# Returned splits tied behind weight casts, one quarter transposed on TensorE, later loads of x and norm rows in a hybrid GLA/Hyena block

## The chip, the core and the metric

The kernel runs on one core of a Trainium2 chip. The metric is the device time of one execution in microseconds (us). Engines are named as in the profile: PE (TensorE), DVE (VectorE), ACT (ScalarE), POOL (GpSimd) and SP (SyncE). Each works through its own instructions in the order in which the program holds them. SP, ACT and POOL also issue DMA transfers.

## The reference

One encoder layer on 256 tokens of width 2048, all in float32. Cut to what matters:

```python
proj = h @ w_in                                  # 2048 -> q, k, v, r, gates, Hyena input, merge gates
y_gla = gla_branch(q, k, v, r, ...)              # gated linear attention in both directions, 4 heads
y_hy = hyena_branch(hy_u, ...)                   # short convolution, then two gated FFT convolutions
g = sigmoid(gate_logits).reshape(B, L, 2, D)
merged = g[:, :, 0] * (y_gla @ w_gla_o) + g[:, :, 1] * (y_hy @ w_hy_o)
h = layernorm(ALPHA * h + merged @ w_out, ln1_g, ln1_b)
ff = square(relu(h @ w_ff1)) @ w_ff2             # 2048 -> 8192 -> 2048
out = layernorm(ALPHA * h + ff, ln2_g, ln2_b)
```

## The kernel before

**Weights.** All weights stream from DRAM in blocks of 128x2048 floats (1 MB). `fetch` (L115) asks for a block on SP's queue (`raw`, three buffers) and splits each of its two halves into a high part (`whi`, a cast on ACT, L108) and a low part (`wlo`, a subtraction on DVE, L109). `whi` and `wlo` have three half-block buffers each, so a cast can run at most one and a half blocks ahead of PE. Activations are split in the same way, and each product is made of three: high x high, high x low, low x high. One block is 24 matmuls of 128x512 for both halves of the tokens. Four blocks are a group (`token_group`, L215) of 512 output columns. Where the result is to lie with channels on the partitions, two blocks make a `channel_pair` (L175).

**Side work.** `later(d, fn)` (L135) notes that `fn` is to be written out `d` blocks from now. `pump` (L139), which comes after each block, writes out what is due, and `drain` (L147) all that is left. So the lines of Hyena, GLA and of the returned data stand between those of the weight blocks. The framework's scheduler then orders each engine's instructions by a plan of its own, unless a dependency fixes it.

**Returns from DRAM.** A matmul's output has tokens on the partitions; the next one needs channels there. `turn_blocks` (L202) transposes 32x32 squares on DVE, `bounce_out` (L205) writes the tile to DRAM and `bounce_in` (L210) reads it back in four DMAs so that the squares land in place; both are on POOL's queue. Then the returned tile is split by a cast on ACT and a subtraction on DVE, `split_hi_lo` (L107). This is done in GLA (`gla_back`, L612), in Hyena (`turned`, L681, with `hy_v`, `hy_out`), for the merged tensor (L826 to L838, `back_split` L821) and for the MLP's hidden tensor f (`ff1`, L1020).

**Stages in order.** Opening and the Hyena filters (`filt_time`, `filt_freq`, beside the products of q, k and r); GLA (beside v and the first merge gate, g1); Hyena in eight channel groups, each with three channel pairs uv, ux and uz, and the output products of GLA, go, in between; the second merge gate, g2; the return of Hyena's result (L815) and its output product ho, which merges into m; the transposed m, mT, times w_out: the groups wo0 to wo3, of which the last runs in an order written out by hand together with the first norm (L961 to L1010); then the MLP, ff1 in four quarters f0 to f3 and ff2, w2, one quarter behind; the second norm and the store.

In Hyena, `hy_fwd` and `hy_mul` make a group's spectrum, multiply it by the filter T, read from DRAM, and split the product into Yh and Yl; `hy_inv` multiplies these with the inverse transform (yp).

**The seam between ho and wo.** `zr` holds x for the residual (z1) and two norm rows. It takes the memory of `yh`, ho's operand, so it is loaded after ho: x in one DMA (L846), two rows of the norm, each spread over all partitions (L851), all on ACT's queue. Each of ho's four groups is multiplied by the gate and added (L832, L833), turned and sent through DRAM. wo0 needs all four quarters, the last one in its fourth block.

Of the kernel before, what the change touches and what calls it, by code (L numbers as in the profile page):

```python
# [10 lines left out]
F32 = mybir.dt.float32  # L11
# [6 lines left out]
P = 128  # L18
# [41 lines left out]
def block_kernel(  # L60
# [45 lines left out]

    def split_hi_lo(hi, lo, src):  # L107
        nc.scalar.copy(hi, src)  # L108
        nc.vector.tensor_tensor(lo, src, hi.bitcast(F32), op=ALU.subtract)  # L109

    nblk = wblk.shape[0]
# [294 lines left out]
    def filt_freq(c, o):  # L406
        def run():
            hh, hl = fst.pop(("h", c, o))

            def transform(r):  # L410
                pt = psum_side(f"F{r}{c}{o}").rearrange("p (a b) -> p a b", a=2)
                for i in range(2):
                    mm3(pt[:, i], dfth[:, 2 * r + i], dftl[:, 2 * r + i], hh[:, r, i], hl[:, r, i], True, True)
                return pt

            t = fp.tile([P, 2, 2, CW], F32, tag="T", name=f"T{c}{o}")
            odd = fp.tile([P, 2, CW], F32, tag="odd", name=f"odd{c}{o}")
            even = transform(0)
            nc.scalar.copy(odd, transform(1))
            nc.vector.tensor_tensor(t[:, 0], even, odd, op=ALU.add)  # L420
# [191 lines left out]
    def gla_back(h, ib):  # L612
# [3 lines left out]
        def run():  # L616
            src = sg.rearrange("p a (k j) -> p k a j", k=4)
            dst = [yT[:, 4 * h:4 * h + 4, i, ib * P:(ib + 1) * P].rearrange("p k (a j) -> p k a j", a=4)
                   for i in range(2)]
            split_hi_lo(dst[0], dst[1], src)  # L620
        return run
# [23 lines left out]
    for g in range(4):  # L645
        pss = token_group(xT, f"g1_{g}")
        for tb in range(NT):
            sig = nc.scalar.activation(m_part(g, tb), pss[tb], AF.Sigmoid)
            dep = mybir.DependencyInfo(mybir.DependencyClass.NoSync, mybir.DependencyReason.DATA)
            tc.add_manual_dep(sig.ins, last_norm[0].ins.name, dep, reason="one table change")  # L650
        for h, ib in ((g, 0), (g, 1)):
# [46 lines left out]
    def hy_v(c):  # L698
        def run():
            zh, zl = z_tiles(f"{c}0")  # L700
            sg = cst.pop(("v", c))
            for tb in range(NT):
                hi, lo = (t[:, tb].rearrange("p (c a j) -> p c a j", c=2, a=4) for t in (zh, zl))
                split_hi_lo(hi, lo, sg[:, tb::2])
            cst[("z", c, 0)] = (zh, zl)
# [39 lines left out]
    def hy_inv(c, o):  # L745
        def run():
# [15 lines left out]
            else:  # L762
                cst[("y", c)] = turned([py.rearrange("p (k b i) -> p b k i", k=4, b=4)], f"y{c}", "sg")
        return run
# [24 lines left out]
    for c in range(NCH):  # L789
        ps = channel_pair(xT, f"uv{c}")  # L790
        cst[("v", c)] = turned(by_parity(short_conv(ps, 2 * c, f"cv{c}", "cv", 2)), f"v{c}", "sg")
        later(3, hy_v(c))
        later(4, hy_fwd(c, 0))
        later(4, hy_mul(c, 0))
        ps = channel_pair(xT, f"ux{c}")
        cst[("x1", c)] = turned(by_parity(short_conv(ps, 16 + 2 * c, f"cx{c}", "cv", 2)), f"x{c}", "x1")
        later(5, hy_inv(c, 0))
        later(6, hy_fwd(c, 1))
        later(6, hy_mul(c, 1))
        ps = channel_pair(xT, f"uz{c}")  # L800
        cst[("x2", c)] = short_conv(ps, 32 + 2 * c, f"cz{c}", "cz", 2)
        later(7, hy_inv(c, 1))
        later(9, hy_out(c))
        for _ in range(go_after[c]):
            gla_o_group()


    g2_sb = qp.tile([P, NT, D], F32, tag="G", name="g2_sb")
# [5 lines left out]
    yhT = act_tile(base, "yT", "yh")  # L814
    for c in range(NCH):  # L815
        yr = hp.tile([P, 2, L], F32, tag="cv", bufs=2, name=f"yr{c}")
        nc.gpsimd.dma_start(yr, yh_dram[c])
        split_hi_lo(yhT[:, 2 * c:2 * c + 2, 0], yhT[:, 2 * c:2 * c + 2, 1], yr)
    mT = act_tile(base, "xT", "mT")

    def back_split(dst, sg):  # L821
        src = sg.rearrange("p a (k j) -> p k a j", k=4)
        hi, lo = (dst[:, :, i].rearrange("p k (a j) -> p k a j", a=8) for i in range(2))
        split_hi_lo(hi, lo, src)

    for g in range(4):  # L826
        pss = token_group(yhT, f"ho{g}")
# [17 lines left out]
    z1 = zr[:, 0:2]  # L845
    nc.scalar.dma_start(z1, x.rearrange("(a p) d -> p a d", p=P))  # L846

    def load_rows(i0):
        rows = zr[:, 2:4]
        for i in range(2):  # L850
            nc.scalar.dma_start(rows[:, i, :], ln_rows[i0 + i:i0 + i + 1, :].broadcast_to([P, D]))  # L851
        return rows
# [43 lines left out]
    st1 = ep.tile([P, NT, 8, 6], F32, tag="bst", bufs=2, name="bst1")  # L896
    rows1 = load_rows(0)

# [121 lines left out]
    def ff1(qi):  # L1020
# [12 lines left out]
        for g in range(1 if qi == 0 else 0, 4):  # L1033
# [200 lines left out]
```

## Time and profile before

| | |
|---|---|
| median of three runs | 1846.69 us (1844.93 to 1849.45) |
| profiled execution: time, span | 1849.45 us, 1847.4 us |
| PE, DVE, ACT, POOL busy | 1822.5, 1285.9, 896.4, 178.4 us |
| mean granted TensorE clock | 0.995 |
| DMA moved | 403.27 MB, 218 GB/s over the span |

A row of a timeline gives start, time, engine, line, operation and tiles; a bracket holds the engine's idle time before it and what ended that. In a table of stretches each engine has its busy time and, behind it, its count of instructions. Matmuls overlap in the pipeline, so the mean time of one in the profile is longer than the distance between two.

### The profile page before, as it was taken

What the parts mean: (1) busy time and instruction counts of PE and PEld (TensorE: products, weight loads), DVE (VectorE), ACT (ScalarE), POOL (GpSimd) and SP (SyncE); (2) the same over time, 40 slices, a digit from 0 to 9 for tenths busy, and PEclk for the clock granted to TensorE, in tenths of its full rate; (3) what the DMA queues carried; (4) which work ended last, traced back from release to release, by engine and by line L of the source; (5) the groups of instructions that cost most, each with busy time, mean ns of one, the idle gap of its engine ahead of it and who ended that gap; (6) DMA issues with size and microseconds to landing.
All of it is one profiled execution on the core that took longest, in us unless ns stands there. A gap on an engine that the chain in (4) does not pass through costs nothing.

```text
span 1847.4 us, 23213 instructions
## 1 busy us (share of the span) xinstructions
PE 1822.5 (99%) x8924; PEld 1529.2 (83%) x8924; DVE 1285.9 (70%) x1659; ACT 896.4 (49%) x1120; POOL 178.4 (10%) x317
## 2 busy tenths in 40 slices
PE   9999999999999999999999899999999999999998
PEld 7888888888888888888888688888888878888887
DVE  6889878965898988988456566566555555565567
ACT  5556567654554555455444444444434443444332
POOL 1000000120121211211001000011100100010000
PEclk9999999999999999999999999999999999999999
DMA  8677654575666666657557763677756765666553
GB/s 293 219 252 272 242 199 151 191 242 187 226 224 220 231 225 214 236 214 251 206 210 239 279 235 127 206 247 236 242 186 209 241 211 184 225 230 225 184 198 119
DMA packets 73631, 403.27 MB, mean 218 GB/s; under 512 B 10928, under 2 KB 13776, under 8 KB 34096
## 3 DMA queue, kind: packets, MB, share of 16 engines
q1 hardware_dynamic: 47376, 324.03, 49.6%
q0 software_dynamic: 19376, 58.62, 10.3%
q10 hardware_dynamic: 6768, 19.14, 3.0%
q8 instruction: 70, 1.15, 0.2%
q14 instruction: 41, 0.34, 0.1%
HBM read 370.82 MB, written 30.93 MB: 217 GB/s over the span
## 4 chain that ended last, share of the span: by engine, by line
PE 78%; DMA 3%; DVE 3%; issue 3%; ACT 1%; POOL 1%; DVEq 0%; ACTq 0%; POOLq 0%
PE w L93 18%; PE f L93 17%; PE g L93 9%; PE ux L93 5%; PE uz L93 5%; PE uv L93 5%; PE go L93 5%; PE v L93 4%; PE wo L93 3%; PE r L93 1%; DMA back<-tr_f 1%; DMA tr_m<-mt 1%; PE Zp L93 1%; PE yp L93 1%; PE ho L93 1%
## 5 line engine op out<-in xcount | busy, mean ns | idle before, releaser
L109 DVE TENSOR_TENSOR wlo<-raw,whi 128x1024 fp32r<-128x1024 f32 (+2 forms) x603 | 725.9, 1208 | 432.1 <-ACT whi L108 425.1
L108 ACT CAST whi<-raw 128x1024 fp32r<-128x1024 f32 (+2 forms) x603 | 627.1, 1042 | 709.6 <-PE w L93 184.0
L93 PE MATMUL w<-whi,f 128*128 128x512 f32 x960 | 296.6, 389 | 1.4 <-ACT whi L108 1.3
L93 PE MATMUL f<-whi,hT 128*128 128x512 f32 x960 | 296.1, 389 | 0.0
L93 PEld LDWEIGHTS w<-whi,f 128*128 128x128 f32 x960 | 180.1, 188 | 39.5 <-ACT whi L108 2.2
L93 PEld LDWEIGHTS f<-whi,hT 128*128 128x128 f32 x960 | 180.2, 188 | 37.4
L93 PE MATMUL w<-wlo,f 128*128 128x512 f32 x480 | 187.0, 389 | 1.4 <-DVE wlo L109 1.4
L93 PE MATMUL f<-wlo,hT 128*128 128x512 f32 x480 | 186.9, 389 | 0.1
L93 PE MATMUL g<-whi,xT 128*128 128x512 f32 x512 | 158.7, 390 | 0.0
L93 PEld LDWEIGHTS g<-whi,xT 128*128 128x128 f32 x512 | 96.1, 188 | 19.8
L93 PEld LDWEIGHTS w<-wlo,f 128*128 128x128 f32 x480 | 90.1, 188 | 20.9 <-DVE wlo L109 2.3
L93 PEld LDWEIGHTS f<-wlo,hT 128*128 128x128 f32 x480 | 90.1, 188 | 19.1 <-DVE wlo L109 0.5
L93 PE MATMUL g<-wlo,xT 128*128 128x512 f32 x256 | 99.7, 390 | 0.0
L93 PE MATMUL r<-whi,xT 128*128 128x512 f32 x256 | 81.4, 391 | 0.0
L93 PE MATMUL v<-whi,xT 128*128 128x512 f32 x256 | 80.1, 391 | 0.0
L93 PE MATMUL go<-whi,yg 128*128 128x512 f32 x256 | 80.1, 390 | 0.0
L93 PE MATMUL ho<-whi,yh 128*128 128x512 f32 x256 | 79.0, 389 | 0.0
L93 PE MATMUL wo<-whi,mT 128*128 128x512 f32 x208 | 66.9, 401 | 7.5 <-ACT whi L108 3.9
L93 PE MATMUL ux<-xT,whi 128*128 128x512 f32 x256 | 65.3, 393 | 0.0
L93 PE MATMUL uz<-xT,whi 128*128 128x512 f32 x256 | 64.8, 392 | 0.0
L93 PE MATMUL uv<-xT,whi 128*128 128x512 f32 x256 | 64.0, 392 | 0.0
L207 POOL DMA_DIRECT2D tr_f<-work x15 | 10.9, 725 | 529.2 <-DVE work L203 529.2
(321 smaller groups left out, 2835.3 us busy)
## 6 DMA issues: line engine op xcount, KB each, us to landing
raw<-wblk SPq DMA_DIRECT2D x302, 1024.0 KB, 4.9
w<-w4s ACTq DMA_DIRECT2D x16, 512.0 KB, 3.5
Td<-T POOLq DMA_DIRECT2D x16, 512.0 KB, 3.9
Tl<-Td POOLq DMA_DIRECT2D x16, 512.0 KB, 4.3
tr_f<-work POOLq DMA_DIRECT2D x15, 512.0 KB, 3.8
back<-tr_f POOLq DMA_DIRECT2D x60, 128.0 KB, 3.7
zr<-ln_rows ACTq DMA_DIRECT2D x4, 1024.0 KB, 13.2
raw<-wblk SPq DMA_DIRECT2D x11, 256.0 KB, 7.4
```

The source lines that it names most:

```text
L93: return eng.tensor.matmul(*args, **kw)
L108: nc.scalar.copy(hi, src)
L109: nc.vector.tensor_tensor(lo, src, hi.bitcast(F32), op=ALU.subtract)
L207: nc.gpsimd.dma_start(td.rearrange("t p x -> p t x"), st)
```

## The change

1. `split_hi_lo` takes `held`. A held split's cast on ACT is tied behind the last weight cast that has been written out so far (`last_cast`): an order within ACT's own instructions, without a semaphore. Held are the splits of data that return from DRAM: GLA's, Hyena's v, Hyena's result, the merged tensor's and f's. The last two are due after three blocks instead of two.
2. The last quarter of the merged tensor, from ho3, no longer goes through DRAM. Eight 128x128 transposes on PE put it into PSUM, and a split from there makes mT.
3. x is loaded in four column quarters, three blocks apart, and the norm rows eight blocks in, each tied behind the last weight cast.
4. Delays in Hyena: forward transforms due after 5 and 7 blocks (4 and 6 before), the output after 11 (9 before); `cz` has three buffers, the returned y its own (`sgy`), the filter tile T two. Hyena's result is read back during g2, not after it.

```diff
+    def behind(ins, other):
+        if other is not None:
+            dep = mybir.DependencyInfo(mybir.DependencyClass.NoSync, mybir.DependencyReason.DATA)
+            tc.add_manual_dep(ins.ins, other.ins.name, dep, reason="in order")
...
+    def split_hi_lo(hi, lo, src, held=False):
+        cast = nc.scalar.copy(hi, src)
+        if held:
+            behind(cast, last_cast[0])
         nc.vector.tensor_tensor(lo, src, hi.bitcast(F32), op=ALU.subtract)
+        return cast
...
-            split_hi_lo(hi, lo, raw[:, h * 1024:(h + 1) * 1024])
+            last_cast[0] = split_hi_lo(hi, lo, raw[:, h * 1024:(h + 1) * 1024])
...
-            t = fp.tile([P, 2, 2, CW], F32, tag="T", name=f"T{c}{o}")
+            t = fp.tile([P, 2, 2, CW], F32, tag="T", bufs=2, name=f"T{c}{o}")
...
-        later(4, hy_fwd(c, 0))
-        later(4, hy_mul(c, 0))
+        later(5, hy_fwd(c, 0))
+        later(5, hy_mul(c, 0))
...
-        later(6, hy_fwd(c, 1))
-        later(6, hy_mul(c, 1))
+        later(7, hy_fwd(c, 1))
+        later(7, hy_mul(c, 1))
...
-        later(9, hy_out(c))
+        later(11, hy_out(c))
...
+    def y_back(c):
+        yr = hp.tile([P, 2, L], F32, tag="cv", bufs=2, name=f"yr{c}")
+        nc.gpsimd.dma_start(yr, yh_dram[c])
+
+        def run():
+            split_hi_lo(yhT[:, 2 * c:2 * c + 2, 0], yhT[:, 2 * c:2 * c + 2, 1], yr, held=True)
+        later(2, run)
...
+    for c in range(NCH):
+        later(max(c, 2 * c - 5) + 2, lambda c=c: y_back(c))
...
-    for g in range(4):
+    for g in range(3):
         pss = token_group(yhT, f"ho{g}")
...
-        later(2, lambda g=g, sg=sg: back_split(mT[:, 4 * g:4 * g + 4], sg))
+        later(3, lambda g=g, sg=sg: back_split(mT[:, 4 * g:4 * g + 4], sg))
+    pss = token_group(yhT, "ho3")
     drain()
+    for tb in range(NT):
+        with tc.high_priority():
+            gp2 = g2_sb[:, tb, 1536:]
+            mp = m_part(3, tb)
+            nc.vector.tensor_tensor(gp2, gp2, pss[tb], op=ALU.mult)
+            nc.vector.tensor_tensor(mp, mp, gp2, op=ALU.add)
+            pt = psum_side(f"mt3{tb}")
+            for k in range(4):
+                nc.tensor.transpose(pt[:, k * P:(k + 1) * P], mp[:, k * P:(k + 1) * P], ident)
+            hi, lo = (mT[:, 12:16, i, tb * P:(tb + 1) * P] for i in range(2))
+            split_hi_lo(hi, lo, pt.rearrange("p (k x) -> p k x", k=4))
...
-    nc.scalar.dma_start(z1, x.rearrange("(a p) d -> p a d", p=P))
+
+    def load_z(g):
+        cs = slice(g * 512, (g + 1) * 512)
+        behind(nc.scalar.dma_start(z1[:, :, cs], x[:, cs].rearrange("(a p) d -> p a d", p=P)), last_cast[0])
+
+    for g in range(4):
+        later(3 * g, lambda g=g: load_z(g))
...
-    rows1 = load_rows(0)
+    rows1 = zr[:, 2:4]
+    later(8, lambda: load_rows(0))
...
-            later(2, lambda g=g, sg=sg, f=f: back_split(f[:, 4 * g:4 * g + 4], sg))
+            later(3, lambda g=g, sg=sg, f=f: back_split(f[:, 4 * g:4 * g + 4], sg))
```

The order on ACT at the seam before; `whi161` is the first block of wo0, `mg` a returned quarter of the merged tensor, `zr` x and the rows:

```order
L108 CAST mT_8868<-mg2_9322 128x4x256
L108 CAST whi161_0_9403<-raw161_9401 128x1024
L108 CAST whi161_1_9407<-raw161_9401 128x1024
L108 CAST whi162_0_9437<-raw162_9435 128x1024
L846 DMA zr_9490<-x 128x2x2048
L854 ACT_TABLE_LOAD
L851 DMA zr_9490<-ln_rows 128x2048 x2
L108 CAST whi162_1_9441<-raw162_9435 128x1024
L108 CAST whi163_0_9503<-raw163_9501 128x1024
L108 CAST whi163_1_9507<-raw163_9501 128x1024
```

The same place of the changed kernel; `mt30` and `mt31` are the two halves of the last quarter in PSUM:

```order
L115 CAST whi161_1_9405<-raw161_9399 128x1024
L115 CAST mT_8868<-mg2_9322 128x4x256
L115 CAST whi162_0_9437<-raw162_9435 128x1024
L115 CAST whi162_1_9441<-raw162_9435 128x1024
L115 CAST whi163_0_9502<-raw163_9500 128x1024
L115 CAST mT_8868<-mt30_9471 128x4x128
L115 CAST whi163_1_9506<-raw163_9500 128x1024
L877 DMA zr_9492<-x 128x2x512
L115 CAST mT_8868<-mt31_9480 128x4x128
L888 ACT_TABLE_LOAD
L115 CAST whi164_0_9537<-raw164_9535 128x1024
```

The third quarter's cast has moved behind one more weight block, the last quarter's cast is fed from PSUM, and where x and both rows stood there is one quarter of x.

On PE in the changed kernel, the transposes stand among wo0's products, after 26 of them (the two rows ahead of them are the 25th and 26th); before, wo0 has no other work in it here:

```order
L93 MATMUL wo0_0_9498<-whi162_0_9437,mT_8868 128x512
L93 MATMUL wo0_1_9499<-whi162_0_9437,mT_8868 128x512
L864 MATMUL mt30_9471<-ident_71,m1_3525 128x128 x4
L93 MATMUL wo0_0_9498<-wlo162_0_9438,mT_8868 128x512
L93 MATMUL wo0_0_9498<-whi162_0_9437,mT_8868 128x512
L93 MATMUL wo0_1_9499<-wlo162_0_9438,mT_8868 128x512
```

Ten products of wo0 lie between the four transposes of `mt30` and those of `mt31`.

In the MLP, ACT's order before, around the return of f2's first group (`f2<-back`) and the relu of its second (`work<-f21`):

```order
L108 CAST whi232_0_12244<-raw232_12242 128x1024
L108 CAST whi232_1_12248<-raw232_12242 128x1024
L108 CAST f2_12055<-back_10319 128x4x256
L108 CAST whi233_0_12280<-raw233_12278 128x1024
L108 CAST whi233_1_12284<-raw233_12278 128x1024
L1037 ACTIVATE work_10318<-f21_0_12206 128x512
```

and after:

```order
L115 CAST whi232_0_12249<-raw232_12247 128x1024
L115 CAST whi232_1_12253<-raw232_12247 128x1024
L115 CAST whi233_0_12283<-raw233_12281 128x1024
L115 CAST whi233_1_12287<-raw233_12281 128x1024
L115 CAST f2_12060<-back_10324 128x4x256
L1072 ACTIVATE work_10323<-f21_0_12211 128x512
```

The returned cast has moved behind the two casts of one more weight block and stands right ahead of the next relu.

More of the change, by code (lines that the diff above doesn't have):

```diff
@@ L619, in run @@
                    for i in range(2)]
-            split_hi_lo(dst[0], dst[1], src)
+            split_hi_lo(dst[0], dst[1], src, held=True)
         return run
@@ L648, in block_kernel @@
             sig = nc.scalar.activation(m_part(g, tb), pss[tb], AF.Sigmoid)
-            dep = mybir.DependencyInfo(mybir.DependencyClass.NoSync, mybir.DependencyReason.DATA)
-            tc.add_manual_dep(sig.ins, last_norm[0].ins.name, dep, reason="one table change")
+            behind(sig, last_norm[0])
         for h, ib in ((g, 0), (g, 1)):
@@ L703, in run @@
                 hi, lo = (t[:, tb].rearrange("p (c a j) -> p c a j", c=2, a=4) for t in (zh, zl))
-                split_hi_lo(hi, lo, sg[:, tb::2])
+                split_hi_lo(hi, lo, sg[:, tb::2], held=True)
             cst[("z", c, 0)] = (zh, zl)
@@ L762, in run @@
             else:
-                cst[("y", c)] = turned([py.rearrange("p (k b i) -> p b k i", k=4, b=4)], f"y{c}", "sg")
+                cst[("y", c)] = turned([py.rearrange("p (k b i) -> p b k i", k=4, b=4)], f"y{c}", "sgy")
         return run
@@ L813, in block_kernel @@
     drain()
[L814 to L818, printed above, removed]
     mT = act_tile(base, "xT", "mT")
@@ L823, in back_split @@
         hi, lo = (dst[:, :, i].rearrange("p k (a j) -> p k a j", a=8) for i in range(2))
-        split_hi_lo(hi, lo, src)
-    for g in range(4):
+        split_hi_lo(hi, lo, src, held=True)
+    for g in range(3):
         pss = token_group(yhT, f"ho{g}")
@@ L850, in load_rows @@
         for i in range(2):
-            nc.scalar.dma_start(rows[:, i, :], ln_rows[i0 + i:i0 + i + 1, :].broadcast_to([P, D]))
+            behind(nc.scalar.dma_start(rows[:, i, :], ln_rows[i0 + i:i0 + i + 1, :].broadcast_to([P, D])), last_cast[0])
         return rows
```

6 lines of the change are left out of this document (3 added, 3 removed).

## The prediction, made before the run

> **What bounds it.** I read the page's busy table first, then the engines' busy time by stretches of 50 us, then who waited for whom on PE, then the timelines of PE and ACT at the places where PE stood still.
>
> ```profile
> PE 1822.5 (99%) x8924; PEld 1529.2 (83%) x8924; DVE 1285.9 (70%) x1659; ACT 896.4 (49%) x1120; POOL 178.4 (10%) x317
> ```
>
> PE is busy for 99% of the span, so only three things can shorten it: fewer matmuls, PE's few stops, or a slow PE clock. The change drops no matmul. So I look for stops. In the stretches below the bracket behind PE's busy time is the count of matmuls, and PEclk is the granted clock.
>
> ```profile
> core 0: us, PE busy (x) PEld busy (x) DVE busy (x) ACT busy (x) POOL busy (x), PEclk, DMA share, GB/s
> 200.00:250.00 50.00, 48.52 (x233) 40.08 (x232) 34.51 (x39) 25.25 (x29) 2.14 (x4) 1.00 0.66 234
> 1000.00:1050.00 50.00, 43.71 (x181) 34.35 (x180) 28.34 (x30) 18.67 (x18) 6.10 (x10) 0.97 0.82 296
> 1050.00:1100.00 50.00, 48.61 (x207) 40.13 (x208) 31.38 (x35) 23.73 (x24) 0.00 (x0) 0.97 0.58 210
> 1200.00:1250.00 50.00, 50.00 (x223) 41.40 (x222) 32.40 (x33) 24.44 (x26) 6.83 (x11) 1.00 0.70 239
> 1450.00:1500.00 50.00, 49.05 (x214) 39.62 (x213) 28.23 (x28) 22.41 (x24) 7.04 (x12) 1.00 0.74 233
> 1500.00:1550.00 50.00, 48.02 (x211) 39.13 (x210) 24.88 (x23) 18.75 (x19) 0.00 (x0) 1.00 0.59 191
> ```
>
> 1200:1250 is an undisturbed stretch of 128x512 products: 223 of them. 1000:1050 gets through 42 fewer, 1050:1100 through 16 fewer, both at a clock of 0.97; 1450:1500 lacks 9 and 1500:1550 lacks 12. These products are all of one shape, so a missing count is lost time. The chain of waits gives the price of one:
>
> ```profile
> 1308.82 87.04 PE w L93 x384
> ```
>
> 87.04/384 is 0.227 us. 1000:1100 therefore loses 58 x 0.227 = 13.2 us, and 1450:1550 21 x 0.227 = 4.8 us. PE's timeline has the stops themselves:
>
> ```profile
> 1041.15 1.22 PE L93 MATMUL wo<-whi,mT 128*128 128x512 f32 x2 [2.76 <-ACT whi L108]
> 1047.10 0.73 PE L93 MATMUL wo<-whi,mT 128*128 128x512 f32 x2 [1.13 <-ACT whi L108]
> 1051.39 0.80 PE L93 MATMUL wo<-whi,mT 128*128 128x512 f32 x1 [3.56 <-ACT mT L108]
> 1507.78 0.73 PE L93 MATMUL w<-whi,f 128*128 128x512 f32 x2 [1.27 <-ACT whi L108]
> 1041.00:1046.00 5.00, 4.78 (x12) 3.07 (x12) 1.23 (x1) 0.10 (x1) 1.64 (x3) 0.66 1.02 364
> 1051.00:1056.00 5.00, 4.61 (x13) 3.72 (x14) 3.52 (x3) 2.33 (x3) 0.00 (x0) 0.66 0.29 123
> ```
>
> The two long stops are followed by a clock of 0.66 over 5 us: each costs another 0.34 x 5 = 1.7 us after it has ended. ACT, which casts the weights, tells why PE stopped:
>
> ```profile
> 1021.63 0.39 ACTq L846 DMA_DIRECT2D zr<-x  x1
> 1022.08 0.94 ACTq L851 DMA_DIRECT2D zr<-ln_rows  x2
> 1034.03 1.05 ACT L108 CAST whi<-raw 128x1024 fp32r<-128x1024 f32 x1 [2.71 <-DMA raw<-wblk]
> 1040.05 1.04 ACT L108 CAST whi<-raw 128x1024 fp32r<-128x1024 f32 x1 [3.29 <-DMA raw<-wblk]
> 1050.29 1.04 ACT L108 CAST mT<-mg 128x1024 fp32r<-128x1024 f32 x1 [3.25 <-DMA mg<-tr_m]
> 1481.42 1.05 ACT L108 CAST f<-back 128x1024 fp32r<-128x1024 f32 x1 [5.14 <-DMA back<-tr_f]
> 1505.73 1.05 ACT L108 CAST f<-back 128x1024 fp32r<-128x1024 f32 x1 [6.29 <-DMA back<-tr_f]
> ```
>
> At 1022 x and two norm rows are asked for at once; the weight blocks behind them come late (1034, 1040), and the last quarter of the merged tensor comes back from DRAM later still (1050). In the MLP the cast of a returned tensor stands in ACT's queue ahead of weight casts and holds them up until it lands.
>
> **The change, part by part.** *The last quarter on TensorE.* The DRAM trip of group 3 goes, and with it the 3.56 us stop. Added are 8 transposes of 128x128. The nearest ones are those of the first norm, four to a row, whose successor's start gives their price:
>
> ```profile
> 1121.45 0.60 PE L49 MATMUL ht<-ident,zr 128*128 128x128 f32 x4
> 1121.81 0.72 PE L49 MATMUL f<-hT,whi 128*128 128x256 f32 x4
> 1135.70 1.09 PE L49 MATMUL ht<-ident,zr 128*128 128x128 f32 x4
> 1136.44 0.78 PE L49 MATMUL f<-hT,whi 128*128 128x256 f32 x2
> ```
>
> 0.36 us for four at full clock, 0.74 at the slow one: 0.7 to 1.5 us for eight, all on PE; I take 0.7, since nothing in the new order should slow the clock there. They wait for DVE, which multiplies and adds first:
>
> ```profile
> 1023.23 1.28 DVE L832 TENSOR_TENSOR g_sb<-g_sb,ho 128x512 f32<-128x512 f32 x2
> 1024.42 1.29 DVE L833 TENSOR_TENSOR m<-m,g_sb 128x512 f32<-128x512 f32 x2
> 1019.81 1.23 DVE L109 TENSOR_TENSOR mT<-mg,mT 128x1024 fp32r<-128x1024 f32 x1 [4.04 <-ACT mT L108]
> ```
>
> With one returned split and one weight split among them (1.23 each) the second half is ready 2 x 1.28 + 2 x 1.23 = 5.0 us after ho3, the first one weight and one addition earlier. The new order sets 26 products (5.9 us) ahead of the first transposes and 36 ahead of the second, so neither waits. Should that cover go, PE stops for what is missing of 5 us, at most. ACT and DVE each trade one long split for two short ones; both have time there (18.67 and 28.34 of 50).
>
> By the Trainium skill, "TensorE: Matmul & The Clock Gate", Part 4 (PE-mode transpose), transposes do not count as activity for the clock. That speaks against this edit: by it the sum would be one slow spell, 1.7 us, worse. The trace leaves it open: the clock was 1.00 in 1450:1550 through a stop of 1.27 us, more than eight transposes take, and fell after one of 2.76.
>
> *Loads of x and the norm rows.* x goes in four quarters, three weight blocks apart, the rows eight blocks in. The 4 MB burst at 1022 becomes 0.5 MB at a time up to the rows, so the waits at 1034 and 1040, hence the stops of 2.76 and 1.13 us, should go. The sizes and landing times by source (KB each, median us):
>
> ```profile
> raw<-wblk SPq DMA_DIRECT2D x302, 1024.0 KB, 4.9
> zr<-ln_rows ACTq DMA_DIRECT2D x4, 1024.0 KB, 13.2
> zr<-x ACTq DMA_DIRECT2D x1, 2048.0 KB, 10.7
> ```
>
> The first quarter waits for ho3's last product to free its slot, which by its place behind whi163_1, three blocks on, is past; it is needed some five half blocks (13 us) after its issue. Behind each issue on ACT's queue stand weight casts, for which PE would wait; an issue costs ACT 0.39 us. With all four causes gone, 1000:1100 gets back its 13.2 us, clock included; the lower bound is the idle time alone, 6.29 + 1.39 = 7.7.
>
> *Returned splits one block later, behind the last cast.* In the MLP the cast of f moves behind two more weight casts, one block, or 24 x 0.227 = 5.4 us. The worst wait is 6.29 us, of which ACT, in step with PE, idles some 1.7 anyway: a cast takes 1.05 of the 2.7 us that PE needs for half a block (12 x 0.227). So 4.6 us is what has to be covered, and 5.4 does it: the 4.8 us go. Next in line is the relu of the next group, behind the moved cast, with a whole group to spare. The same edit on the merge's, GLA's and Hyena's splits I cost at nothing: 450:830 below has PE busy for all 380 us, so their waits lie under PE already.
>
> *Two T buffers.* The one DVE wait in the filter stage that reached PE:
>
> ```profile
> 203.69 0.69 DVE L420 TENSOR_TENSOR T<-F,odd 128x512 f32<-128x512 f32 x1 [4.09 <-DMA Td<-T]
> ```
>
> A second buffer removes it, and with it 200:250's idle 1.5 us; nothing at worst.
>
> *Hyena's delays, cz, sgy, y_back.* No instruction is added. y_back's loads still wait on POOL's queue for the splits that free their two buffers, and the last y return and store still stand behind some of them; ho needs the result several blocks later. I take nothing for these; what the shorter delays cost if their cover goes is the last rival.
>
> Sum: 13.2 + 4.8 + 1.5 - 0.7 = 18.8 us. The profiled execution took 1849.45 us (span 1847.4 and 2.05 around it): 1830.6. It is the slowest of three, 2.8 above the median, so some of its stops may be missing from the others; against that stand small new waits wherever the scheduler has moved work. I let these cancel: **1831**.
>
> **Rivals.** *A, the rows collide later.* Rows and the last quarter of x, 2.5 MB, now fall into the third output group, beside the weights and a resident block. For it: the 4 MB at 1022 cost 2.76 + 1.13 = 3.9 us of stops and two slow spells. Against: it is smaller, and no quarter waits on a return there. In proportion 2.5/4 x 3.9 = 2.4 and one slow spell: 1831 + 2.4 + 1.7 = 1835; in full 3.9 + 3.4: 1838. Chance 0.12. The Trainium skill, "DMA: Bandwidth & Descriptors" (Queues, rings and completion order), has each engine take turns between the queues that have work; by that any size of burst doubles a weight block's landing while it lasts, which is this rival. No run here shows the new place.
>
> *B, the transposes slow the clock*, by the rule above: one or two spells, 1832.7 to 1834.4. Chance 0.06.
>
> *C, the change does not do what it says.* The tie is only an order on one engine, no wait and no speed-up of the return. If returns take over 5.4 us longer than their new place allows, the MLP's 4.8 us stay: 1836. The margin of 0.8 us is thin. Chance 0.08.
>
> *D, slower: DVE starves Hyena's inverse transform.* Forward transforms are due one block later, inverse ones as before, so three blocks between them become two. All weights, too, pass DVE there:
>
> ```profile
> 450.00:830.00 380.00, 380.00 (x2187) 334.98 (x2186) 338.76 (x488) 198.74 (x270) 70.35 (x127) 1.00 0.65 223
> 620.82 1.22 DVE L109 TENSOR_TENSOR Yl<-Z,Yh 128x1024 fp32r<-128x1024 f32 x1
> 625.66 0.28 PE L93 MATMUL yp<-Yl,dih 128*128 128x256 f32 x1
> ```
>
> DVE is busy for 89%. The operand is ready 625.66 - 622.04 = 3.6 us ahead of its product. If the shorter interval makes it 3.6 + w late at each of 16 products, PE loses 16 w; from w = 1.3 on (21 us) the kernel is slower than before, and at 2 it takes 1863. Against: the products are placed by the scheduler, not at their due time. Chance 0.04.
>
> **Numbers.** A measurement can tell 0.3%, 5.5 us: faster is below 1841.2, slower above 1852.2. Forecast 0.70, A 0.12, B 0.06, C 0.08, D 0.04. A and C together with a part of the unknown costs reach past 1841: 0.05 of their 0.20. So faster 0.91, same 0.05, slower 0.04. The range: down, the median's 2.8 and the slow clock of the first norm (its spell, below, costs 0.38 x 9 = 3.4), should that shift away, 1831 - 6.2 = 1825; up, A in full and one slow spell more, 1840.
>
> ```profile
> 1133.00:1142.00 9.00, 9.00 (x44) 8.51 (x44) 6.24 (x8) 3.18 (x4) 0.00 (x0) 0.62 0.18 56
> ```
>
> **What would show it.** Right: PE's waits list has no wo<-mT and no wo<-whi of microseconds; the stretches after ho3 count some 223 matmuls at clock 1.00; no f cast waits over 1.7 us with PE idle behind it. Wrong: raw waits on ACT in the third output group (A); a clock of 0.66 right after the mt3 transposes (B); w<-whi stops around a return (C); yp waiting for Yl (D).

## The result, and the profile after

| | before | changed |
|---|---|---|
| median (range), runs | 1851.94 us (1842.43 to 1856.12), 19 | 1837.01 us (1828.89 to 1847.14), 19 |
| profiled execution: time, span | 1849.45, 1847.4 us | 1832.63, 1830.5 us |
| mean granted TensorE clock | 0.995 | 0.997 |

The ratio of the changed kernel to the one before is 0.9929, with a 95% interval of 0.991 to 0.9948. It is 0.7% faster: 15 us in the medians, 16.8 us between the two profiled executions; forecast were 18.8 us and 1831 us. What has to be explained is less the gain than two other things: the ordinary run of the changed kernel is 4.4 us longer than its profiled one, and its runs lie 18 us apart.

The stretches of the changed kernel, with the columns that the prediction's stretches have:

```profile
200.00:250.00 50.00, 50.00 (x240) 41.67 (x239) 35.73 (x41) 27.87 (x32) 2.14 (x4) 1.00 0.63 228
1000.00:1050.00 50.00, 50.00 (x226) 41.39 (x225) 34.14 (x38) 24.52 (x25) 3.05 (x5) 1.00 0.73 240
1050.00:1100.00 50.00, 50.00 (x223) 41.40 (x222) 29.89 (x34) 20.57 (x20) 0.00 (x0) 1.00 0.81 305
1450.00:1500.00 50.00, 50.00 (x222) 41.44 (x221) 30.70 (x30) 21.97 (x23) 6.11 (x10) 1.00 0.76 239
1500.00:1550.00 50.00, 50.00 (x222) 41.40 (x222) 24.45 (x22) 19.81 (x19) 0.00 (x0) 1.00 0.55 199
```

PE is busy without a gap in all of them. 1000:1100 now holds 449 matmuls, 8 of which are the transposes: 441 - 388 = 53 more products, 53 x 0.227 = 12.0 us. 1450:1550 holds 444 - 425 = 19 more, 4.3 us. 200:250 gained its 1.5 us. That makes 17.8; the opening gave back 1.9 (PE waited 2.7 + 1.3 us for `open` here, 2.1 before), which leaves 15.9 of the 16.8 named.

What PE and then ACT waited for (us in total, times, longest):

```profile
PE open L93 <- DVE xT L118: 2.7, 2, 2.1
PE open L93 <- ACT whi L115: 1.3, 1, 1.3
ACT whi L115 <- DMA raw<-wblk: 14.4, 8, 4.7
ACT f L115 <- DMA back<-tr_f: 6.0, 6, 1.6
```

The rest of PE's list are waits of the opening, of v and of the two norms, none of more than 1.9 us in total; no wo and no w is left on it. ACT still waits for weight blocks, up to 4.7 us, and PE does not feel it: the casts run ahead. The longest wait for a returned f is 1.6 us, 6.29 before. But the returns themselves did not become faster. Two DMA rows of the changed kernel (KB each, median us to landing), and below them the same two before:

```profile
tr_f<-work POOLq DMA_DIRECT2D x15, 512.0 KB, 5.9
back<-tr_f POOLq DMA_DIRECT2D x60, 128.0 KB, 5.5
```

```profile
tr_f<-work POOLq DMA_DIRECT2D x15, 512.0 KB, 3.8
back<-tr_f POOLq DMA_DIRECT2D x60, 128.0 KB, 3.7
```

f's write to DRAM takes 5.9 us in place of 3.8, its reading back 5.5 in place of 3.7. The queues show what moved. Before, POOL asked for a write and SP 0.84 us later for a block of weights:

```profile
1444.26 0.72 POOL L207 DMA_DIRECT2D tr_f<-work  x1 [14.66 <-DVE work L203]
1445.10 0.33 SPq L120 DMA_DIRECT2D raw<-wblk  x1
```

In the changed kernel the order of the two depends on the place. Below are a first write of a quarter, asked for 0.92 us ahead of the weights, and a second one, 0.89 us behind them; the line under each pair is its landing time, from a query of that one write:

```profile
1409.18 0.72 POOL L217 DMA_DIRECT2D tr_f<-work  x1 [97.56 <-DVE work L213]
1410.10 0.33 SPq L130 DMA_DIRECT2D raw<-wblk  x1
DMA to landing us min/median/max: 3.7/3.7/3.7
1431.86 0.33 SPq L130 DMA_DIRECT2D raw<-wblk  x1
1432.75 0.72 POOL L217 DMA_DIRECT2D tr_f<-work  x1 [16.99 <-DVE work L213]
DMA to landing us min/median/max: 5.5/5.5/5.5
```

Moving the cast by one block has shifted the loads of weights against the writes, and a write that comes behind a load takes some 2 us longer. This holds in all fourteen profiled executions: of 69 writes asked for 0.89 us behind a load, 65 took 5.4 to 6.6 us (the other four, beside a load of norm rows, 9.5 to 10.5), and of 125 asked for 0.8 to 0.95 us ahead of one, 124 took 3.5 to 4.6 us. Why the phase shifts (which buffer the load waits for) the runs do not tell.

### The profile page after: what moved, and what is told of

It reads as the page before. It is cut to its first block, busy times and chain, and to the rows that moved or that the text cites. A ratio compares the mean times of both kernels' runs of the same rounds, so it can differ in the third digit from the quotient of the medians.

```text
span 1830.5 us, 23221 instructions
## 1 busy us (share of the span) xinstructions
PE 1816.1 (99%) x8932; PEld 1528.8 (84%) x8932; DVE 1281.9 (70%) x1658; ACT 898.5 (49%) x1121; POOL 175.0 (10%) x312
## 4 chain that ended last, share of the span: by engine, by line
PE 96%; DVE 2%; DMA 0%; ACT 0%; issue 0%; SPq 0%; DVEq 0%; ACTq 0%
PE w L93 19%; PE f L93 19%; PE g L93 10%; PE uz L93 5%; PE ux L93 5%; PE uv L93 5%; PE r L93 5%; PE go L93 5%; PE ho L93 5%; PE wo L93 4%; PE v L93 4%; PE k L93 2%; PE q L93 2%; PE yp L93 1%; PE Zp L93 1%; PE F L93 1%
## 5 line engine op out<-in xcount | busy, mean ns | idle before, releaser
L217 POOL DMA_DIRECT2D tr_f<-work x15 | 10.9, 725 | 517.7 <-DVE work L213 517.7
```

What stands on the lines that cost most here:

```text
L217: nc.gpsimd.dma_start(td.rearrange("t p x -> p t x"), st)
```

## The experiments

Two theories went into them. *Additive*: the terms of the prediction hold each by itself (seam 13 us, MLP 5, everything else 1 to 2). *Rival*: the terms depend on each other, since what one stop frees, another takes back. All kernels ran in five rounds; the ratio is to the kernel before on the same chip, and the runs of before have medians of 1852.0, 1853.0 and 1854.7 us in the three groups of four (e1 to e4, e5 to e8, e9 to e12; each group ran on a chip of its own). Where two kernels of different groups are compared below, the ratios are the safer measure.

| kernel | median us (range), runs | ratio, 95% interval |
|---|---|---|
| e1 seam only | 1850.38 (1839.11 to 1858.73), 12 | 0.9981 [0.995, 1.0011] |
| e2 MLP only | 1852.99 (1846.71 to 1860.89), 12 | 0.9996 [0.9969, 1.0022] |
| e3 one burst | 1836.51 (1827.98 to 1845.97), 12 | 0.992 [0.9895, 0.9945] |
| e4 quarter by DRAM | 1836.84 (1831.24 to 1847.16), 8 | 0.9923 [0.9892, 0.9955] |
| e5 rest only | 1844.15 (1838.1 to 1851.05), 12 | 0.9951 [0.9926, 0.9975] |
| e6 one T | 1836.95 (1830.13 to 1841.82), 7 | 0.9906 [0.9871, 0.9941] |
| e7 rows2 early | 1837.39 (1834.09 to 1841.86), 6 | 0.9914 [0.9882, 0.9947] |
| e8 rows2 early, due 4 | 1830.84 (1829.05 to 1833.64), 6 | 0.9878 [0.9846, 0.991] |
| e9 = e8 without the rest | 1835.77 (1832.29 to 1839.93), 6 | 0.9906 [0.9871, 0.994] |
| e10 = e8 without the seam | 1837.26 (1836.65 to 1840.43), 8 | 0.9918 [0.9889, 0.9946] |
| e11 = e8 without the MLP's tie | 1840.64 (1832.45 to 1843.36), 9 | 0.9909 [0.9875, 0.9942] |
| e12 MLP with four blocks only | 1847.15 (1842.43 to 1851.78), 12 | 0.9965 [0.9944, 0.9986] |

**e1, the seam alone**: the kernel before with the transposed quarter and the tied loads, and nothing else (mT's other quarters due after two blocks and untied, as before).

```diff
-    for g in range(4):
+    for g in range(3):
         pss = token_group(yhT, f"ho{g}")
...
-    rows1 = load_rows(0)
+    rows1 = zr[:, 2:4]
+    later(8, lambda: load_rows(0))
```

> The kernel before with the edits at the seam between ho and wo alone: last quarter transposed on PE, x in four quarters, norm rows late. Own theory (each edit removes PE's stops at its own place, and the savings add up): no stop of microseconds in the 100 us around the seam and a clock of 1.00 there; 12.5 us less than the kernel before (13.2 less 0.7 for the transposes), ratio 0.993; the stops of the MLP stay. Rival (the gain comes from the shifted Hyena and filter work, not from the seam): the ratio stays within 0.3% of 1.

A miss: a ratio of 0.9981, where 0.993 was expected; the rival's number came, but not for its reason, as the rows show. The stretches, ACT's wait for f, and the timelines of ACT and PE:

```profile
1000.00:1050.00 50.00, 50.00 (x225) 41.19 (x225) 34.34 (x40) 23.68 (x25) 3.04 (x5) 1.00 0.69 234
1250.00:1300.00 50.00, 45.37 (x189) 36.55 (x188) 26.57 (x26) 19.42 (x22) 6.88 (x12) 0.93 0.68 214
ACT f L115 <- DMA back<-tr_f: 49.2, 12, 9.4
1212.89 0.97 ACTq L879 DMA_DIRECT2D zr<-ln_rows  x2
1259.50 1.04 ACT L115 CAST f<-back 128x1024 fp32r<-128x1024 f32 x1 [9.42 <-DMA back<-tr_f]
1261.54 1.22 PE L93 MATMUL f<-whi,hT 128*128 128x512 f32 x2 [4.40 <-ACT whi L115]
```

The seam is clean (225 products at clock 1.00 in 1000:1050, against 181), and the time is lost 200 us later: 1250:1300 holds 33 products fewer than an undisturbed stretch, 7.5 us with the slow clock behind the stop of 4.40 us. A part of that may be the change's own doing. `load_rows` serves the second norm too, so its tie moved the second pair of rows, 2 MB, from the first norm (before, at 1139 us) to 1213 us; the write of f that follows at 1215 us took 11.4 us, in the changed kernel 9.7. PE's stop of 4.40 us belongs to the next return, whose write at 1241 us was asked for 0.89 us behind a load and took 6.5 us. That the first delay led to the second is argued, not shown: e1 with these rows untied was not run, and e5 below loses 7.2 us in f and w without this collision.

**e2, the MLP alone**: the kernel before with f's splits tied and due after three blocks.

```diff
-            later(2, lambda g=g, sg=sg, f=f: back_split(f[:, 4 * g:4 * g + 4], sg))
+            later(3, lambda g=g, sg=sg, f=f: back_split(f[:, 4 * g:4 * g + 4], sg, held=True))
```

> The kernel before with the returned splits of the MLP alone tied behind the last weight cast and due after three blocks. Own theory: the stops of w behind whi and wlo go, those at the seam stay; 4 to 5 us less, ratio 0.9975. Rival (the tie is only an order, the return itself is what is late, so the wait moves on with it): PE still stops behind a cast of f, ratio 1.000.

A miss as well: 0.9996, though the interval reaches down to 0.9969 and so does not exclude the 0.9975 that was expected. The write of f is slow here too, and the seam's stops stand as before (PE waits 4.5 + 3.0 us there):

```profile
tr_f<-work POOLq DMA_DIRECT2D x15, 512.0 KB, 5.8
```

So the slow write comes with the third block, not with the seam. The rival's stops behind a cast of f are not in this profiled execution, which has 0.9 us of PE's waits in f and w; it is the slowest of the twelve runs and lost its time ahead of the MLP.

**e3 and e4, halves of the seam undone** in the changed kernel: x and the first rows in one burst, or the last quarter through DRAM.

```diff
-    for g in range(4):
-        later(3 * g, lambda g=g: load_z(g))
+    nc.scalar.dma_start(z1, x.rearrange("(a p) d -> p a d", p=P))
```

```diff
-    for g in range(3):
+    for g in range(4):
         pss = token_group(yhT, f"ho{g}")
```

> The changed kernel, but x in one DMA and both norm rows at once after ho, as before the change. Own theory (two causes at the seam, the burst and the DRAM trip): weight blocks land in 10 to 11 us again, ACT waits for raw some 3 us each, PE stops for about 3.9 us in wo0 and the clock falls to half once: 5.6 us more than the changed kernel, about 9 less than before. Rival (the DRAM trip of the last quarter was the only cause, the weight blocks were late for other reasons): no stop, the time of the changed kernel.

> The changed kernel, but the last quarter of the merged tensor goes through DRAM as before. Own theory (each cause has its own stop): the trip takes some 17 us from ho3's end without the burst beside it, PE has 16 to 19 us of other products, so a stop of 0 to 2 us is left, and the 0.7 us of transposes go: within 2 us of the changed kernel. Rival (the transposes are what pays): PE stops 3.6 us for mT and a slow clock follows, 5 us more than the changed kernel.

Both took the changed kernel's time, 1836.5 and 1836.8 us, so e3's own theory missed and e4's held. Of e3 a stretch at the seam, one in the MLP, ACT's wait for f and the landing of weight blocks at the seam (1017:1045); of e4 PE's waits at the seam:

```profile
1000.00:1050.00 50.00, 50.00 (x226) 41.32 (x225) 34.33 (x38) 23.97 (x25) 3.04 (x5) 1.00 0.79 297
1300.00:1350.00 50.00, 47.48 (x201) 38.52 (x200) 28.84 (x28) 22.30 (x23) 3.04 (x5) 0.97 0.59 193
ACT f L115 <- DMA back<-tr_f: 41.0, 11, 6.2
raw<-wblk SPq DMA_DIRECT2D x5, 1024.0 KB, 6.3
```

```profile
PE wo L93 <- ACT whi L115: 1.1, 1, 1.1
PE wo L93 <- ACT mT L115: 0.9, 1, 0.9
```

With the burst, and without the trip through DRAM, PE does not stop at the seam at all: 4 MB at once stop nothing by themselves here. With the trip, and without the burst, PE waits 2.5 us (0.5 of it for `wlo`). In the median, weight blocks landed in 6.3 and 5.4 us in these two kernels, in 11.1 us before. Both keep the ties and later places of the merged quarters' splits; e10 below has burst, trip and these ties. And e3's profiled execution, 10 us above that of the changed kernel, has its stops in the MLP, around the casts of f.

**e5, the rest alone**: the changed kernel with the seam as before and the MLP's splits untied and due after two blocks. Left are the second T buffer, GLA's and Hyena's ties and delays, `y_back`, and the merged quarters' splits, tied and due after three blocks.

> The changed kernel without its seam edits (the loads of x and of the first two norm rows go back to one burst, the last merged quarter goes back through DRAM) and without the tie and the third block in the MLP: what is left is the second T buffer, the ties and later due places of the GLA and Hyena splits, the loads of Hyena's output spread over the gates, and the merged quarter's splits tied and due a block later. Additive theory (the record of the prediction: seam 13 us and MLP 5 us in the profiled execution, the rest about 1 us): the stops at the seam and in the MLP are there as before, so a ratio of 0.999 to 1.000, about 1849 us. Theory of the hidden part (since the seam alone gave a ratio of 0.998 and the MLP part alone 1.000, and since taking a half of the seam out of the changed kernel cost nothing, the remaining edits carry most of the gain in ordinary runs): a ratio of 0.993 to 0.995, 1836 to 1840 us. Theory of parts that only act together (each stop that goes is given back at another place that still stops): a ratio of 0.997 to 1.000 with the stops of its profile in the MLP or at the seam adding to over 15 us.

1844.15 us: 8.9 us below before's 1853.0, where 1 to 2 us had been forecast. The ratio of 0.9951 lies just outside the range of the theory of the hidden part. Its profiled execution is one of its longer ones and shows what the rest does not cover:

```profile
ACT f L115 <- DMA back<-tr_f: 54.5, 12, 6.0
PE wo L93 <- ACT mT L115: 2.5, 1, 2.5
PE wo L93 <- ACT whi L115: 2.4, 2, 1.3
```

PE's waits at the seam for a cast are 4.9 us instead of 7.5 (3.9 + 3.6 before), and none is over 2.5.

**e6, one T buffer** in the changed kernel.

```diff
-            t = fp.tile([P, 2, 2, CW], F32, tag="T", bufs=2, name=f"T{c}{o}")
+            t = fp.tile([P, 2, 2, CW], F32, tag="T", name=f"T{c}{o}")
```

> The changed kernel with a single T buffer in the filter phase. The prediction held the second buffer worth 1.5 us, the waits of TensorE there. Additive theory: the waits on T come back, a ratio to before of 0.993 to 0.994 where the changed kernel has 0.993, 1 to 2 us above the changed kernel. Theory of the hidden part, if the second buffer is what carries it: the ratio rises to 0.996 or more, 7 us above the changed kernel.

1836.95 us: the buffer is not the hidden part. Its stop does come back in the profile, in its old size, and is lost in the spread of the runs:

```profile
206.63 0.50 PE L93 MATMUL r<-wlo,xT 128*128 128x512 f32 x1 [1.50 <-DVE wlo L118]
```

**e7 and e8, the MLP's returns.** e7 is the changed kernel with the second pair of rows untied; e8 has a fourth block as well.

```diff
-            behind(nc.scalar.dma_start(rows[:, i, :], ln_rows[i0 + i:i0 + i + 1, :].broadcast_to([P, D])), last_cast[0])
+            ld = nc.scalar.dma_start(rows[:, i, :], ln_rows[i0 + i:i0 + i + 1, :].broadcast_to([P, D]))
+            if i0 == 0:
+                behind(ld, last_cast[0])
```

```diff
-            later(3, lambda g=g, sg=sg, f=f: back_split(f[:, 4 * g:4 * g + 4], sg))
+            later(4, lambda g=g, sg=sg, f=f: back_split(f[:, 4 * g:4 * g + 4], sg))
```

> The changed kernel with only the load of the second pair of norm rows (2 MB) left untied, as before: it starts again in the norm phase and not behind a weight cast in the MLP's first blocks, where its write collided with a return trip of f0 (17.7 to 20.8 us in the profiles, 12.3 before). Theory of the collision: the trip at 1215 us falls back under 14 us, no stop is left at 1230 to 1240 us, and 0 to 2 us are gained in typical runs: a ratio of 0.991 to 0.993. Rival (the trip has 16 us of cover with its third block, so the collision costs nothing): the same ratio as the changed kernel within 0.0015. Other rival (the early load lengthens the norm phase, where weight blocks wait for queue room): a ratio of 0.994 to 0.995.

> As the run before it, and the splits of the MLP's returned data come due after four blocks of weights, not three: 5 us more cover for trips that take up to 19 us. Theory that late trips still stop TensorE in the MLP in ordinary runs (12 us in the profile of the kernel with one burst): a ratio of 0.987 to 0.991, about 1833 us or below. Rival (with three blocks the trips are covered in most runs, and what differs from run to run is elsewhere): the same ratio as with three blocks, 0.991 to 0.994. Other rival (a fourth block puts the split past its first reader): TensorE waits for f, 3 us or more for each of eight quarters, a ratio of 0.998 or above.

e7 gains nothing that shows, though the return at 1214 us takes 15.0 us there and not 18.9. e8 is the fastest kernel of the study: 6.6 us below e7 in the medians, on the same chip and with ranges that do not overlap. Its six runs lie 4.6 us apart, those of e7 7.8. Its DMA rows and, on the two queues, a write with its load:

```profile
tr_f<-work POOLq DMA_DIRECT2D x15, 512.0 KB, 3.6
back<-tr_f POOLq DMA_DIRECT2D x60, 128.0 KB, 4.2
1429.14 0.72 POOL L217 DMA_DIRECT2D tr_f<-work  x1 [15.27 <-DVE work L213]
1430.07 0.33 SPq L130 DMA_DIRECT2D raw<-wblk  x1
```

The write is ahead of the load again and takes 3.6 us, and ACT's list of waits has no row for a returned f. So the ordinary run of the changed kernel lost some 6 us to returns that its own profiled execution did not show. The profiled executions bear that out. With three tied blocks PE's waits in f and w come to 0 (changed), 0.9 (e2), 8.6 (e3), 0 (e4), 2.7 (e6) and 3.4 us (e7); with four tied blocks (e8, e9, e10, e12) there is none in any of the four.

**e9 to e12, the parts with f's returns covered.** e9 is the kernel before with the seam edits, the second rows early and f's splits tied and due after four blocks; e10 is e8 with the seam as before; e11 is e8 with `held=False` on f's splits alone; e12 is the kernel before with only f's splits changed:

```diff
-            later(2, lambda g=g, sg=sg, f=f: back_split(f[:, 4 * g:4 * g + 4], sg))
+            later(4, lambda g=g, sg=sg, f=f: back_split(f[:, 4 * g:4 * g + 4], sg, held=True))
```

> The kernel with four blocks and early second norm rows, the best so far (1830.84 us in six runs, before 1852 us), without the middle part: one T buffer, no ties and no later due places on the GLA and Hyena splits, Hyena's output loaded and split behind the gates, and the merged quarter's splits due after two blocks without a tie. The seam edits and the MLP tie with four blocks stay. Theory that the middle part carries most of what the two named parts do not (it gave a ratio of 0.995 alone): 6 to 9 us slower than the best, 1837 to 1840 us, a ratio of 0.992 to 0.994, with the lost time in the profile before 1050 us or on the merged quarter's splits. Additive theory of the prediction's record (seam 13 us, MLP 5 us, the middle 1.5 us): 1832 us, a ratio of 0.989.

> The best so far without the seam edits: the loads of x and of the first norm rows go back to one burst and the last merged quarter goes back through DRAM; the middle part and the MLP tie with four blocks stay. If the seam edits are worth in ordinary runs what the prediction's record gave them (13 us): 1843 to 1845 us, a ratio of 0.995 to 0.996. If the middle part's tie on the merged quarters has already taken a part of those stops (7 us were left in the profile of the middle part alone): 1836 to 1839 us, a ratio of 0.991 to 0.993. If either half of the seam is enough only because the other stays, this one, without both, shows the stop of TensorE at 1035 to 1055 us again, 6 us or more.

> The best so far with the splits of the returned data due after four blocks but not tied behind a weight cast: the planner puts each split two blocks of casts further ahead on ScalarE than with the tie (and all else is the same). Theory that the place in the order does it, and that a due place without the tie gives no place: ScalarE waits for the returned data again (over 20 us in sum in the profile, against 0 to 1 us for the best) and the time is 4 to 10 us above the best, 1835 to 1841 us, a ratio of 0.990 to 0.994. Rival (what counts is that the write to DRAM no longer meets a load of weights, which the tie does not set): the same as the best within 1.5 us, writes of 3.6 to 3.9 us.

> The kernel before with only the MLP's splits tied and due after four blocks, not three. With three blocks alone the ratio was 0.9996: the third block moved a load of weights onto the moment of the write to DRAM, which then took 5.5 to 6.4 us in place of 3.6 to 3.9. Theory of that collision: with four blocks the write takes 3.6 us again, no stop is left in the MLP, and the MLP part is worth its 5 to 7 us: 1845 to 1847 us, a ratio of 0.996 to 0.997. Rival (the MLP part is worth nothing alone, since whatever it frees is lost at the seam or in Hyena): a ratio of 0.998 or more.

With f's returns covered, the medians form a table of the other two parts (e8 ran in another group than the three others; before had 1853.0 us there, 1854.7 here):

| | seam as before | seam changed |
|---|---|---|
| rest as before | 1847.15 (e12) | 1835.77 (e9) |
| rest changed | 1837.26 (e10) | 1830.84 (e8) |

The seam is worth 11.4 us alone and 6.4 on top of the rest; the rest 9.9 alone and 4.9 on top of the seam. They overlap by 5 us (by the ratios the four are 10.9, 7.4, 8.7 and 5.2 us, and the overlap 3.5). The two steps from e12 are clear of the spread, since neither range reaches e12's; the two steps to e8 are not, since the intervals of the ratios overlap. PE's waits at the seam in e10 come to 3.8 us, none over 1.7; e9 has none at the seam, but the T buffer's stop, 1.5 us at two places; those of e12 have the seam as it was (7.8 us), beside a short write of 3.7 us. The waits and the landing of weight blocks at the seam (1017:1045) of e10, then the two stretches of e12 and of e10:

```profile
PE wo L93 <- ACT whi L115: 2.8, 2, 1.7
PE wo L93 <- DVE wlo L118: 1.0, 2, 0.5
raw<-wblk SPq DMA_DIRECT2D x5, 1024.0 KB, 10.5
```

```profile
1000.00:1050.00 50.00, 43.05 (x180) 34.13 (x178) 27.91 (x30) 18.35 (x18) 6.09 (x10) 0.95 0.84 298
1050.00:1100.00 50.00, 48.63 (x207) 40.14 (x208) 31.38 (x35) 23.84 (x24) 0.00 (x0) 0.95 0.57 208
1000.00:1050.00 50.00, 46.11 (x188) 36.62 (x187) 27.51 (x29) 19.86 (x20) 6.09 (x10) 0.93 0.81 296
1050.00:1100.00 50.00, 50.00 (x222) 41.42 (x221) 35.95 (x43) 23.90 (x24) 0.00 (x0) 1.00 0.62 228
```

e12 has 387 products there and e10 410, so the rest gives back 23 x 0.227 = 5.2 us at the seam itself, which is the size of the overlap. And with burst and trip together the weight blocks land in 10.5 us again, in place of 6.3 with the burst alone: what e10 still loses at the seam takes the two together.

e12 against e2 is the fourth block against the third, with nothing else changed: 1847.15 against 1852.99 us on different chips, with intervals that overlap from 0.9969 to 0.9986. Against before, the MLP part is worth 6.5 us by the ratio with four blocks (interval 2.6 to 10.4) and nothing measurable with three. e12 and e10 came out as expected, e9 between its two theories. e11 has short writes and no tie; the waits of ACT and PE (its write has 3.7 us):

```profile
ACT f L115 <- DMA back<-tr_f: 32.5, 10, 6.8
PE f L93 <- ACT whi L115: 1.7, 1, 1.7
```

So a due place without the tie is none: the scheduler put the casts two blocks further ahead, and ACT waits for f again, as expected. In the medians that costs 9.8 us, by the ratios 0.003 or 6 us, and the intervals of the ratios overlap: the waits are shown, their price only roughly. e11 has the short write without the later place, and that alone does not do it; the later place with a long write was not run.

## Why the prediction was right, and where it was not

**The seam, 13.2 us: right in its size, wrong in its parts.** The profile gave back 12.0 of 12.5 with the transposes, and e9 against e12 has 11.4 us. But the prediction let the burst cause 2.76 + 1.13 us of stops and the trip 3.56, each by itself. e3 and e4 show that, with the merged quarters' splits tied, the burst stops nothing when no quarter goes through DRAM, and that the trip without the burst costs some 2.5 us. And of the loss at the seam e10 shows 5.2 us to go by the rest alone, which the prediction had at nothing. The halves were not run with the splits untied.

**The transposes, 0.7 us: right.**

```profile
1026.46 0.60 PE L864 MATMUL mt<-ident,m 128*128 128x128 f32 x4
1026.81 0.48 PE L93 MATMUL wo<-wlo,mT 128*128 128x512 f32 x1
```

0.35 us for the first four by the successor's start, 0.36 for the other four at 1029 us, and PE waited for neither. The clock stayed at 1.00 in this stretch, so rival B is out. The rule of the Trainium skill, "TensorE: Matmul & The Clock Gate", Part 4 (PE-mode transpose), that transposes do not count as activity, is not contradicted by that: 0.7 us of them, with products on both sides, had no effect on the clock here (1.00 in 1000:1050).

**The MLP, 4.8 us: right in the profiled execution (4.3), wrong for the ordinary run.** The step that failed is "4.6 us is what has to be covered, and 5.4 does it". It held fixed both the return's time and the write's place. In the table, cover is the time from asking for a write to the cast of its return, at places where ACT waits for nothing, and a trip is the time from asking for the write until the last of its four readings has landed; both are read from the traces.

| us | cover | trip: median, longest | PE's waits in f and w |
|---|---|---|---|
| before | 10.4 | 11.7, 15.5 | 2.7 |
| changed | 14.0 | 13.6, 18.9 | 0 |
| e7 (three blocks) | 14.0 | 13.1, 18.4 | 3.4 |
| e8 (four blocks) | 21.3 | 10.7, 13.7 | 0 |
| e11 (four, untied) | 10.4 | 11.9, 16.1 | 3.1 |

The moved cast shifted the loads of weights onto the writes. So most writes were asked for later against their casts, and the cover rose by 3.6 us where 5.4 had been counted; the trips grew by 2.0 us in the median. That leaves 1.6 us (three of the fifteen writes, asked for ahead of a load, have a cover of 15.5 to 15.9). Only e8's trips stay far inside their cover. That is rival C in its mechanism, late returns that keep the MLP's stops, for which the prediction had "the margin of 0.8 us is thin" and a chance of 0.08. Its price shows in e8 against e7, 6.6 us; e2 alone does not show it.

**The ties in GLA and Hyena, `y_back` and the merge, at nothing: wrong.** Together with the T buffer they are worth 4.9 to 9.9 us. The buffer's stops come to 1.0 to 4.5 us in the six profiled executions with one T, though e6 shows no price in its time. The argument was that PE was busy for all 380 us of 450:830, and that was one execution; and 5.2 us of the gain lie outside that stretch, at the seam. e2's profiled execution, with Hyena as before, has stops that the profile of before did not have:

```profile
PE ho L93 <- ACT whi L115: 2.8, 1, 2.8
PE Zp L93 <- ACT zh L115: 2.2, 1, 2.2
PE F L93 <- DVE T L431: 3.0, 2, 1.5
```

Behind the first, ACT had waited 7.83 us for the return of a merged quarter, which came in time in one run and late in another; behind the second, DVE had waited 6.52 us for a write of Hyena's output; the third is the single T buffer, at two places. All five profiled executions without the rest have some stop of this kind ahead of the seam; of the nine with it none has, but for e6's T. Which edit takes out which stop was not run one by one. That the rest's 5.2 us at the seam come from the merged quarters' splits is likely, not shown: in e12 ACT waits 3.71 us for the third quarter at 1018 us, in e10 not at all.

**"I let these cancel": they did not quite.** The forecast's sum was 1830.6 us. From before's median the parts as measured make 1851.9 - 11.4 (seam) - 4.9 (rest) = 1835.6 us, with nothing for the MLP; 1837.0 was measured. Against the forecast 1835.6 is 2.5 us more for a profiled execution that lay below the median of 19 runs, 4.8 for the MLP and 1.1 for the seam, less 3.4 by which the rest was worth more than the T buffer's 1.5. The range held by luck: two mis-sized terms had opposite signs, and without those 3.4 us the measured 1837.0 would have been 1840.4, outside 1825 to 1840.

**The rivals.** A, the rows colliding in the third output group: 1050:1100 moves 305 GB/s and PE has no gap. A load did collide, but the other pair of rows, in the MLP, where the prediction had not followed `load_rows` to its second call. The write of 11.4 us beside 2 MB of rows agrees with the rule of the Trainium skill, "DMA: Bandwidth & Descriptors" (Queues, rings and completion order), that each engine takes turns between the queues with work; taken out alone (e7) it changed nothing that could be measured. D, Hyena's inverse starved by DVE: PE is busy throughout there.

```profile
450.00:830.00 380.00, 380.00 (x2184) 335.05 (x2183) 335.69 (x487) 200.88 (x273) 72.86 (x132) 1.00 0.66 225
```

## What to carry to other kernels

Where side work waits for transfers, one profiled execution shows which stops happened, not which can happen; compare the landing times with the cover, place by place, and look at the spread of the runs, which here went from 7.8 us to 4.6 (six runs each, e7 and e8) when f's returns were covered. A cast that is moved by one block moves the load behind it as well, so look at what the queues hold at the new moment before counting the block as cover. And test parts on a version whose other stops are gone: on the kernel before the seam looked worthless alone (0.9981, with the second rows tied), with f's returns covered it was worth 6 to 11 us.

## What the runs showed of the hardware

- A 512 KB write to DRAM landed in 3.5 to 3.8 us in the pairs above when it was asked for 0.8 to 0.9 us ahead of a 1 MB load on another queue, in 5.5 us when 0.9 us behind one, and in 9.7 to 11.4 us beside 2 MB more (changed kernel and e1).
- With the 4 MB burst 297 GB/s were moved over 50 us with no stop of PE (e3), where before, at 296 GB/s, PE was idle for 6.3 of 50 us; so a high rate alone says nothing of a stop.
- The same stop can slow PE's clock or not. Before, the 1.5 us stop for T left 200:250 at 1.00; in e6 the same stop at the same place has a stretch at 0.97, and right behind it, in 208:210, a clock of 0.50. e6's row:

```profile
200.00:250.00 50.00, 48.49 (x224) 39.74 (x224) 33.87 (x39) 24.66 (x28) 2.13 (x4) 0.97 0.58 209
```

So a stop is not priced by its length alone: 224 matmuls where before has 233 are, at the 50/240 = 0.208 us of one in this stretch of the changed kernel, 9 x 0.208 = 1.9 us more for the same wait.
